# A two-layer conv / RG-LRU / pooling backbone on one core: modulation sums per column group, blocks turned by VectorE, and a new order in the first head

## The chip, the core and the metric

The kernel runs on one core of a Trainium2 chip. The core has five engines, each with a queue of its own: TensorE (PE, matrix products; its weight loads are shown apart as PEld), VectorE (DVE), ScalarE (ACT), GpSimd (POOL) and SyncE (SP, which here issues nearly all DMA transfers). They work side by side and wait for each other through semaphores. SBUF is the working memory with 128 partitions, PSUM the memory that PE writes its products to. The metric is the device time of one execution in microseconds (us); three runs are given by their median.

## The reference

1024 latent tokens and 256 context tokens of width 1024 pass an even layer (convolution branch and RG-LRU branch), then the latents pass an odd layer (pooling mixer). All data are float32. Each layer starts with an RMS norm and a modulation by vectors made from the conditioning `c` (for the context from `c_ctx`):

```python
shift, scale, gate = jnp.split(silu(c) @ mod_w[l] + mod_b[l], 3, axis=-1)
hx = rmsnorm(x, norm_g[l]) * (1 + scale) + shift       # latents
hc = the same for ctx with silu(c_ctx)                 # first layer only
z  = hx @ w_in                       # split in va, vg, ga, xb, gb
y_a = silu(layernorm(conv31(va * sigmoid(vg)))) * silu(ga)
u = conv4(xb); r, i = sigmoid(u @ w_r + b_r), sigmoid(u @ w_i + b_i)   # per head
y_b = (scan forwards + scan backwards, from the context's last states) * silu(gb)
x = x + gate * (concat(y_a, y_b) @ w_out)
```

The change concerns how `shift` and `scale` of the first layer are computed, how `hx` is formed from them, and the order of the work in the first of the eight heads of the even layer.

## The kernel before

**Layout.** Everything lies feature-major: a tile has 128 features on the partitions and tokens along the free side, so x is eight tiles `xs[k]` of 128x1024, used in two halves of 512 tokens. A product is exact to about float32 by splitting each operand into a high part (a cast to the matmul's reduced float32 type, `wh`, `gh`, `h0h`) and a low part (what is left, `wl`, `gl`, `h0l`), and adding high x high, high x low and low x high: three matmuls per tile (`mm3_steps`, line 153; `mm3_fixed`, line 686).

**Opening (lines 294 to 665).** Here the order on every engine is written by hand. `mm` (line 133) chains all matmuls, `load` (line 123) chains all DMA issues on SP, and `A` and `V` (class `Written`, line 106) chain the operations of ACT and VectorE. So each engine runs its work in the order of the program text, and an instruction that waits holds up what is behind it.

PE's opening work is the fold: eight products `fold_all(n, 0)` and `fold_all(n, 1)`, 24 matmuls each pair, which prepare weights of the second layer (`wfold`) and depend on the weights alone. ACT casts a weight (`cast`), VectorE takes its low part (`low`), ACT copies the product out of PSUM (`fold_copy`), and SP stores it (`fold_store`). Between the folds the inputs are prepared:

- `x_square` and `x_add` sum the squares of x; `ms` (a 128x32 stationary of ones, on four groups of 32 PSUM partitions) and `rx` make the row of reciprocal roots, which stays in two PSUM banks.
- The modulation sums. `cpad` holds silu of `c` and `c_ctx` as columns 0 and 1 of 32 (the rest zero), for each of eight tiles k of the contraction. PE's 128 output partitions are used as four groups of 32, each with its own stationary.
- `x_scale(k)` multiplies x by the scale and `rx` (VectorE, two halves), `x_high(k)` adds the shift and rounds (ACT), `x_low(k)` makes the low part (VectorE).

The sums go in four groups b of two feature tiles. `mod_load(b)` loads four blocks of `modW`; in `mod_mm(b)` the four partition groups share the contraction: group i takes tiles k = i and k = 4 + i, so each group ends with a partial sum for all columns. `mod_row(b)` copies the 128x512 result to SBUF (ACT), and `mod_turn(b)` is four matmuls with the copied row as stationary and a constant selector (`col(O_SEL, 2)`, two columns of `small`), which add the four partial sums and put features on partitions in one step (`modt`). `mod_cols(b)` adds the bias and makes `m0` (shift, scale and, later, gate, for both conditionings) and `a0` (norm gain times 1 + scale).

After the folds comes the first product, `xb0` = tile 0 of `xb`, 48 matmuls in two halves. On PE's queue, 39 matmuls into it, stands one that sums the context's squares (`ms_c`, line 634, tile `ssqc`), for which VectorE adds seven `csq` tiles after the last `x_low`. Then `cx` (the context) is normalised and modulated, and split into `cth` and `ctl` by ACT and VectorE. Still in the opening, `decay_exp` runs on ACT, and six gate dots on VectorE: a row block of `modT` times `cL` (silu of `c` on all partitions), summed along the free side into `m0`.

**Heads (lines 907 to 1000).** The order is again fixed on each engine, by `on` (line 670). In head j PE runs `vg` (two halves), in head 0 the context part `xc` of `xb`, `va` (two halves), the context part of the next `xb`, then the gate products of this head mixed with the next `xb`. ACT makes `first_tap`, VectorE `other_taps` of the 4-wide convolution into `uc`; `uh` and `ul` are its high and low part. `raw_split` (line 705) splits the next weights: high part on ACT, low part on POOL. `fill(n)` lets VectorE go on with the 31-wide convolution of a finished head; in head 0 there is none to go on with until the two products `u` = va * sigmoid(vg) exist. In head 0 the last two gate dots, the bias of the gates and `decay_rates` (26 small POOL operations and a reciprocal, for `chalf` and `cneg`, which the recurrence of the next head uses) come between `ul` and `va`. The splits of the next weight and of the gate weight stand behind these lines:

```python
            cast(uh, uc)
            act(sg[1], vg[1], AF.Sigmoid)
            fill(2)
            vec(nc.vector.tensor_tensor, out=ul, in0=uc, in1=uh.bitcast(F32), op=sub)
```

**Afterwards** come the products `gb` and `wob`, layer norm, `ga`, and the second layer (from line 1345 on), where a planner orders the instructions of each engine by priority and its own estimate of time, with a few orders given by hand.

Of the kernel before, what the change touches and what calls it, by code (L numbers as in the profile page):

```python
# [44 lines left out]
O_SEL = O_FG + KT  # L45
N_SM = O_SEL + 2

NB = 4
KB = KT // NB
MC = KB * P  # L50
# [6 lines left out]
def body(ctx, tc, xT, ctxT, cc, ccol, modT, modW, win, gw, wout, wu, grp, wg, wo1, small, edge, ident, outT):  # L57
# [136 lines left out]
    def decay_exp(act):  # L194
        act.activation(sa, lam, AF.Abs)
        act.activation(sa, sa, AF.Exp, scale=-1.0)
# [97 lines left out]
    with ExitStack() as sctx:  # L294
# [88 lines left out]
        modraw, modr, rows, modt = {}, {}, {}, {}  # L383

        def mod_load(b):
            for q in range(4):
                modraw[b, q] = dtile(f"modw_{b}_{q}") if b < 3 else ctile(f"modw_{b}_{q}", F32)
                load(modraw[b, q], modW[b, q])

        def mod_mm(b):  # L390
            modr[b] = psum(f"modr_{b}")
            for q in range(4):
                j, half = divmod(q, 2)
                for i in range(4):
                    mm(modr[b][32 * i : 32 * i + 32, j * MC : (j + 1) * MC], cpad[:, 4 * half + i],
                       modraw[b, q][:, i * MC : (i + 1) * MC], start=(q == 0), stop=(q == 3), skip_group_check=True)

        def mod_row(b):
            rows[b] = ttile(f"modrow_{b}")
            A.copy(rows[b], modr[b])  # L400

        def mod_turn(b):
            modt[b] = psum(f"modt_{b}")[:, : 4 * KB].rearrange("p (m c) -> p m c", c=2)
            for m in range(2 * KB):
                mm(modt[b][:, m], rows[b][:, m * P : (m + 1) * P], col(O_SEL, 2), start=True, stop=True)

        def mod_cols(b):
            for j in range(2):
                ms = slice(j * KT + KB * b, j * KT + KB * (b + 1))
                V.tensor_tensor(out=m0[:, :, ms], in0=modt[b][:, KB * j : KB * (j + 1)].rearrange("p m c -> p c m"),  # L410
                                in1=col(O_MB + ms.start, KB).unsqueeze(1).to_broadcast([P, 2, KB]), op=add)
            for k in range(KB * b, KB * (b + 1)):
                mod_scale(m0, a0, 0, k, V)
# [3 lines left out]
        def x_scale(k):  # L417
            for h in range(2):
                v = xs[k][:, HALF[h]]
                V.scalar_tensor_tensor(out=v, in0=v, scalar=a0[:, 0, k : k + 1], in1=rx[h], op0=mult, op1=mult)  # L420
# [1628 lines left out]
```

## Time and profile before

| what | us |
|---|---|
| median of 3 runs (1283.83 to 1284.45) | 1284.26 |
| the profiled execution | 1282.08 |
| its span, first to last instruction | 1280.3 |
| PE busy in the span | 1258.5 |
| DVE busy | 1134.8 |
| ACT busy | 654.9 |
| POOL busy | 296.9 |

All times inside the trace count from the start of the span. In the profile's lines L116 is the helper through which ACT and VectorE are chained in the opening, L137 the one for matmuls, L127 the one for DMA issues, and L674 the one for the heads, so operations are told apart by the tile that they write (left of `<-`) and read (right of it): `modr` and `modt` are the modulation's sums and turns, `modw` its weights, `x<-x,a,rx` is `x_scale`, `h0h` and `h0l` are `x_high` and `x_low`, `mod<-mod,cL` is a gate dot, `xbc` the context part of `xb`. In brackets stands how long the engine was idle before the line, and what ended that. A float32 matmul of the modulation (not split) shows as two records. In the chain of waits each piece of time is put down to what released the next.

### The profile page before, as it was taken

What the parts mean: (1) busy time and instruction counts of PE and PEld (TensorE: products, weight loads), DVE (VectorE), ACT (ScalarE), POOL (GpSimd) and SP (SyncE); (2) the same over time, 40 slices, a digit from 0 to 9 for tenths busy, and PEclk for the clock granted to TensorE, in tenths of its full rate; (3) what the DMA queues carried; (4) which work ended last, traced back from release to release, by engine and by line L of the source; (5) the groups of instructions that cost most, each with busy time, mean ns of one, the idle gap of its engine ahead of it and who ended that gap; (6) DMA issues with size and microseconds to landing.
All of it is one profiled execution on the core that took longest, in us unless ns stands there. A gap on an engine that the chain in (4) does not pass through costs nothing.

```text
span 1280.3 us, 16129 instructions
## 1 busy us (share of the span) xinstructions
PE 1258.5 (98%) x5822; PEld 1038.9 (81%) x5822; DVE 1134.8 (89%) x1747; ACT 654.9 (51%) x955; POOL 296.9 (23%) x173
## 2 busy tenths in 40 slices
PE   9999999999999999999999999999999999999997
PEld 7787888888888888888887878788888888788786
DVE  7789999999999999988959958999999987887876
ACT  8544566656666533237435346644343444644642
POOL 0005464446444557433210023000000000000003
PEclk9999999999999999999999999999999999999998
DMA  9961121112121234442418565334333334868723
GB/s 374 373 239 50 42 75 42 66 41 75 42 82 42 82 124 135 153 140 83 164 46 291 175 206 172 108 123 157 122 102 132 115 123 132 277 227 282 275 73 132
DMA packets 78704, 182.27 MB, mean 142 GB/s; under 512 B 7712, under 2 KB 23328, under 8 KB 78624
## 3 DMA queue, kind: packets, MB, share of 16 engines
q1 hardware_dynamic: 69632, 176.53, 39.7%
q10 hardware_dynamic: 8992, 4.72, 1.3%
q8 instruction: 45, 0.74, 0.2%
q14 instruction: 35, 0.29, 0.1%
HBM read 137.18 MB, written 44.04 MB: 142 GB/s over the span
## 4 chain that ended last, share of the span: by engine, by line
PE 63%; DVE 19%; DMA 8%; issue 3%; ACT 3%; POOL 2%; SPq 0%; POOLq 0%; ACTq 0%; DVEq 0%
PE wob L674 7%; PE fold L137 5%; DVE conv L674 5%; PE xb L674 4%; PE va L674 4%; PE vg L674 4%; DVE l L674 3%; PE g L674 3%; PE ga L674 2%; PE ga L158 2%; PE ga L160 2%; PE ga L159 2%; PE gb L674 2%; DMA yr_b<-y_b 1%; PE qb_g L1142 1%
## 5 line engine op out<-in xcount | busy, mean ns | idle before, releaser
L674 DVE SCALAR_TENSOR_TENSOR conv<-u,sm,conv 128x505 f32<-128x505 f32 (+6 forms) x224 | 153.7, 745 | 1.0
L1782 POOL TENSOR_TENSOR o<-x,rr 128x256 f32<-128x256 f32 (+1 forms) x10 | 9.7, 1005 | 443.1 <-ACT rr L1782 440.3
L674 ACT ACTIVATE l<-g,sm 128x512 f32<-128x512 f32 (+1 forms) x96 | 58.5, 618 | 57.6 <-PE g L674 57.0
L674 POOL TENSOR_TENSOR l<-l,l 128x1280 f32<-128x1280 f32 x16 | 47.1, 2964 | 25.6 <-ACT l L674 15.1
L674 PE MATMUL gb<-h0h,wl_gb 128*128 128x512 f32 x128 | 49.9, 390 | 0.3 <-POOL wl_gb L674 0.3
L674 PE MATMUL va<-h0h,wl_va 128*128 128x512 f32 x128 | 49.9, 390 | 0.2 <-POOL wl_va L674 0.2
L674 PE MATMUL gb<-h0h,wh_gb 128*128 128x512 f32 x128 | 49.9, 390 | 0.0
L674 PE MATMUL gb<-h0l,wh_gb 128*128 128x512 f32 x128 | 49.9, 389 | 0.0
L674 PE MATMUL va<-h0h,wh_va 128*128 128x512 f32 x128 | 49.8, 389 | 0.0
L674 PE MATMUL va<-h0l,wh_va 128*128 128x512 f32 x128 | 49.8, 389 | 0.0
L674 PE MATMUL wob<-ybl,wh_wob 128*128 128x512 f32 x128 | 49.8, 389 | 0.0
L674 PE MATMUL wob<-ybh,wl_wob 128*128 128x512 f32 x128 | 49.8, 389 | 0.0
L674 PE MATMUL wob<-ybh,wh_wob 128*128 128x512 f32 x128 | 49.8, 389 | 0.0
L674 DVE TENSOR_TENSOR_SCAN l<-l,l 128x256 f32<-128x256 f32 (+1 forms) x32 | 48.7, 1522 | 1.1
L674 DVE SCALAR_TENSOR_TENSOR conv<-cL,wsum,conv 128x506 f32<-128x506 f32 (+3 forms) x70 | 48.1, 744 | 0.2
L674 POOL TENSOR_TENSOR l<-l,uc 128x1280 f32<-128x1280 f32 x16 | 47.7, 3001 | 0.0
L103 ACT CAST wq_wo<-wr_wo 128x512 fp32r<-128x512 f32 x48 | 28.7, 620 | 36.6 <-DMA wr_wo<-wo 17.9
L103 ACT CAST wq_g<-wr_g 128x512 fp32r<-128x512 f32 x48 | 28.2, 620 | 35.7 <-DVE wr_g L1120 16.8
L104 POOL TENSOR_TENSOR wl_wu<-wr_wu,wh_wu 128x1024 fp32r<-128x1024 f32 x8 | 19.2, 2396 | 110.8 <-ACT wh_wu L103 110.8
L674 PE MATMUL xb<-h0l,wh_xb 128*128 128x512 f32 x112 | 43.8, 391 | 0.0
L674 PE MATMUL xb<-h0h,wh_xb 128*128 128x512 f32 x112 | 43.8, 391 | 0.0
L674 PE MATMUL vg<-h0l,wh_vg 128*128 128x512 f32 x112 | 43.6, 389 | 0.0
(619 smaller groups left out, 4357.4 us busy)
## 6 DMA issues: line engine op xcount, KB each, us to landing
modw<-modW SPq DMA_DIRECT2D x16, 512.0 KB, 10.4
x_part<-xp SPq DMA_DIRECT2D x32, 256.0 KB, 2.3
mod<-modT SPq DMA_DIRECT2D x32, 256.0 KB, 4.1
wr_v<-wfold SPq DMA_DIRECT2D x16, 512.0 KB, 4.1
wr_g<-wg SPq DMA_DIRECT2D x16, 512.0 KB, 4.4
wr_wo<-wo SPq DMA_DIRECT2D x16, 512.0 KB, 4.3
mod<-modT SPq DMA_DIRECT2D x14, 512.0 KB, 4.9
yr_t<-y_t SPq DMA_DIRECT2D x14, 512.0 KB, 6.4
```

The source lines that it names most:

```text
L103: return (nc.scalar.copy(hi, src), eng.tensor_tensor(out=lo, in0=src, in1=hi.bitcast(F32), op=sub))
L104: eng.tensor_tensor(out=lo, in0=src, in1=hi.bitcast(F32), op=sub))
L137: m = nc.tensor.matmul(*args, **kw)
L158: mm(ps, hi[:, kc], xh[k][:, cols], start=(k == 0), stop=False)
L159: mm(ps, hi[:, kc], xl[k][:, cols], start=False, stop=False)
L160: mm(ps, lo[:, kc], xh[k][:, cols], start=False, stop=(k == ks - 1))
L674: last[eng] = f(*args, **kw)
L1142: mm = nc.tensor.matmul(ps, lo, xh[k], start=False, stop=(k == KH - 1), skip_group_check=not first)
L1782: tail[eng] = f(*args, **kw)
```

## The change

It has three parts.

1. **Whole sums per column group.** Each partition group of PE now owns 32 of the 128 columns of a feature tile and runs over all eight k, so its sum is whole. `modr` then holds, in group i, column block i in row 0 (`c`) and row 1 (`c_ctx`); turning each 32x32 block puts features on partitions. VectorE does that straight from PSUM (`V.transpose`), so the ACT copy, the four selector matmuls, the selector's columns and four PSUM tiles go. The groups are now two, two and four feature tiles (three groups instead of four): 32, 32 and 32 matmuls with 128, 128 and 256 moving columns, where there were four times 16 with 256. The third group's sums run in three pieces between folds. `modW` is laid out anew: 16 blocks of 512 KB as before. On SP, `fold_store(0)` moves ahead of blocks 8 to 11; `w_load(6)` stays between block 11 and block 12.
2. **Last inputs by halves.** For tiles 4 to 7 the first token half of `x_scale`, `x_high` and `x_low` is made for all four tiles ahead of the last folds, the second half after them. `x_high` and `x_low` of tiles 1 and 3 move ahead of the following fold pieces; `fold_copy` and the casts of weights 6 to 8 stand at new places between them.
3. **First head.** The last operations of the opening's ACT and VectorE chains are now linked to the head's. `ctx_split`, `decay_exp` and the split of `va`'s weight follow `first_tap`; the six opening dots are issued in the head (two after `other_taps`, one between `uh` and `ul`, three after `ul`), the last two with the bias and `decay_rates` after the two `u`. The next weight and the gate weight `gw` are split ahead of `uh`. The loads of `modT` keep their order on SP.

```diff
+        def mod_mm(b, qs):
+            k0, n = ((0, 2), (2, 2), (4, 4))[b]
+            w = n * 64
+            if b not in modr:
+                modr[b] = psum(f"modr_{b}")
+            for q in qs:
+                for e in range(4 // n):
+                    k = (q % 4) * 2 + e if n == 2 else q - 8
+                    for i in range(4):
+                        c = (4 * e + i) * w
+                        mm(modr[b][32 * i : 32 * i + 32, :w], cpad[:, k], modraw[q][:, c : c + w],
+                           start=(k == 0), stop=(k == KT - 1), skip_group_check=True)
 
         def mod_cols(b):
+            k0, n = ((0, 2), (2, 2), (4, 4))[b]
+            t = ttile(f"modt_{b}")[:, : n * 64]
+            V.transpose(out=t, in_=modr[b][:, : n * 64])
...
+        for q in range(4, 8):
+            mod_load(q)
+        fold_store(0)
+        for q in range(8, 12):
+            mod_load(q)
+        w_load(6)
+        for q in range(12, 16):
+            mod_load(q)
...
-        mod_mm(0)
-        mod_row(0)
-        fold_all(4, 1, 0, 1)
-        mod_turn(0)
-        fold_store(0)
-        w_load(6)
-        mod_load(3)
+        mod_mm(0, range(4))
         mod_cols(0)
         x_scale(0)
         x_scale(1)
         x_high(0)
-        fold_all(4, 1, 1, 4)
+        fold_all(4, 1)
         fold_copy(4, 1)
+        x_high(1)
         x_low(0)
...
+        mod_mm(2, range(12, 14))
         fold_all(6, 0, 0, 2)
+        mod_mm(2, range(14, 16))
         mod_cols(2)
         cast(A, 7)
+        fold_all(6, 0, 2, 4)
+        x_scale(4, (0,))
+        x_high(4, HALF[0])
+        x_scale(5, (0,))
+        fold_copy(6, 0)
+        x_high(5, HALF[0])
+        x_low(4, HALF[0])
         low(7)
...
         fold_all(7, 0)
+        for k in range(4, 8):
+            x_scale(k, (1,))
+            x_high(k, HALF[1])
+            if k == 4:
+                fold_copy(7, 0)
+            else:
+                x_low(k - 1, HALF[1])
+        x_low(7, HALF[1])
         fold_all(7, 1)
...
+                fill(2)
+            first_tap(j, xb, uc[:, C:])
+            if state is None:
+                ctx_split()
+                decay_exp()
                 wva = raw_split(raw_va0, "va0")
             other_taps(j, xb, uc[:, C:], 1)
+            if state is None:
+                for m in range(2):
+                    gate_dot(2 * KT + m, gate_raw[m])
...
             if state is None:
                 for m in range(3 * KT - 2, 3 * KT):
+                    gate_raw.append(L[m % 6][:, :D])
+                    nc.sync.dma_start(gate_raw[-1], modT[0, m])
+                cast(uh, uc)
+                act(sg[1], vg[1], AF.Sigmoid)
+                gate_dot(2 * KT + 2, gate_raw[2])
+                vec(nc.vector.tensor_tensor, out=ul, in0=uc, in1=uh.bitcast(F32), op=sub)
+                for m in range(3, 6):
+                    gate_dot(2 * KT + m, gate_raw[m])
...
             whole_[0] = j + 1
+            if state is None:
+                for m in range(3 * KT - 2, 3 * KT):
+                    gate_dot(m, gate_raw[m - 2 * KT])
+                vec(nc.vector.tensor_tensor, out=m0[:, 0, 2 * KT :], in0=m0[:, 0, 2 * KT :],
+                    in1=col(O_MB + 2 * KT, KT), op=add)
+                decay_rates()
```

More of the change, by code (lines that the diff above doesn't have):

```diff
@@ L398, in mod_row, with mod_load @@
[L398 to L405, printed above, removed]
+        modraw, modr = {}, {}
+        def mod_load(q):
+            modraw[q] = dtile(f"modw_{q}") if q < 12 else ctile(f"modw_{q}", F32)
+            load(modraw[q], modW[q])
```

164 lines of the change are left out of this document (61 added, 103 removed).

## The prediction

> **What bounds the kernel now.** I read the page first, then busy time by stage, then the chain of waits through the first 110 us, and last the timelines of the engines there.
>
> ```profile
> span 1280.3 us, 16129 instructions
> PE 1258.5 (98%) x5822; PEld 1038.9 (81%) x5822; DVE 1134.8 (89%) x1747; ACT 654.9 (51%) x955; POOL 296.9 (23%) x173
> ```
>
> Busy time by stage (columns: stretch, its length, busy time of PE, weight loads, DVE, ACT, POOL, granted clock, DMA share, GB/s):
>
> ```profile
> 0.00:60.00 60.00, 57.78 (x380) 44.71 (x381) 45.55 (x79) 41.20 (x60) 0.20 (x4) 1.00 0.98 374
> 60.00:90.00 30.00, 30.00 (x144) 24.87 (x142) 25.47 (x37) 17.55 (x25) 2.30 (x1) 1.00 0.80 294
> 90.00:120.00 30.00, 27.03 (x134) 22.80 (x134) 28.10 (x41) 10.31 (x17) 12.20 (x29) 1.00 0.14 45
> ```
>
> PE bounds the kernel: it is idle 22 us in 1280. Everything that the change touches lies before 120 us. There PE idles only at the start and between 90 and 120 us; what else can be won must be matmul time. So a microsecond counts only if PE executes it or waits for it. The clock is full in all three stretches. In the first one the DMA engines are as full as PE (0.98).
>
> Chain of waits (start, length, what):
>
> ```profile
> 25.66 0.57 PE ms_x L137 x16
> ...
> 33.04 1.86 PE modr L137 x32
> 34.90 0.91 PE fold L137 x3
> 35.81 0.85 PE modt L137 x8
> 36.66 2.19 PE fold L137 x9
> ...
> 51.77 1.86 PE modr L137 x32
> ...
> 54.53 0.87 PE modt L137 x8
> 55.40 8.97 PE fold L137 x39
> 64.38 8.99 PE xb L137 x39
> 73.36 0.45 PE ms_c L137 x2
> ```
>
> Four modulation sums (modr) and four turns (modt) stand on PE in the chain, between fold matmuls, ahead of the first product xb.
>
> PE's own timeline in the first head (start, length; what it waited for in brackets):
>
> ```profile
> 89.70 0.40 PE L674 MATMUL va<-h0l,wh_va 128*128 128x512 f32 x1
> 90.31 0.50 PE L674 MATMUL va<-h0h,wl_va 128*128 128x512 f32 x1 [0.21 <-POOL wl_va L674]
> ...
> 100.97 0.28 PE L674 MATMUL xbc<-ctl,wh_xb 128*128 128x256 f32 x1
> 104.00 0.39 PE L674 MATMUL xbc<-cth,wl_xb 128*128 128x256 f32 x1 [2.75 <-POOL wl_xb L674]
> ```
>
> Here are the two other stalls: PE waits for POOL's low parts of two weights, wl_va and, much longer, wl_xb.
>
> **The change part by part.** I count in PE time, negative for a gain.
>
> *Turns leave PE: -3.37.* The four modt runs go (first and last above, 0.85 and 0.87; with the two between them 3.37). VectorE's block transposes replace them. The before trace has none; its nearest rows are VectorE operations from PSUM on 512 columns (0.68 each, below) for blocks of 128, 128 and 256 columns. I take 0.2, 0.2 and 0.4, between a fixed 0.1 and the full 0.68. They follow modr directly, so ACT's four copies of modr and the second trip through PE are gone as well, and the last one delays the x steps by 0.4 at most. [...]
>
> *Narrower sums: +0.84.* Columns streamed are equal: 64 matmuls of 256 before, 64 of 128 and 32 of 256 after. Before, 32 records take 1.86, or 58 ns each. The shape of the new 128-wide ones (32 stationary columns, 128 moving) is that of ms_x: 16 records in 0.57, 36 ns each. Two groups of 64 such records are 4.56, the third (64 of 58 ns) is 3.72; together 8.28 against 4x1.86 = 7.44. Ends: 0 if only columns count, +3.7 if each narrow record costs a wide one's 58 ns. I take ms_x, which is the same shape.
>
> [...]
>
> *Fewer breaks: -0.55.* Twelve folds beside a modr and a modt take 0.91+2.19 = 3.10, where 8.97/39 = 0.23 each makes 2.76; a break costs some 0.18. Eight go down to five, since group 2 runs in three pieces. Ends: -1.0 to 0.
>
> *The transfers hold part of it: +0.45.*
>
> ```profile
> 24.12 9.69 SPq L127 DMA_DIRECT2D modw<-modW  x8
> ...
> 37.32 4.25 SPq L127 DMA_DIRECT2D modw<-modW  x4
> ...
> DMA to landing us min/median/max: 9.3/10.4/10.8
> ```
>
> The first four blocks are in by then; these rows are the issues of blocks 4 to 11 and 12 to 15, then the time from issue to landing. Issues take up to the landing of older ones, as the DMA engines are full: block 11 goes out at 33.5 and lands near 43.9, block 15 goes out at 41.2 and lands near 51.6. Before, PE came for that group at 51.77: just in time. The change leaves the bytes ahead of it the same (it only moves fold_store(0) ahead of blocks 8 to 11, and w_load(6) stays behind those), so it still lands at 51.6, while PE would now reach that block at 51.4; blocks 8 to 11 land one store later (512 KB, 1.4 us at 374 GB/s), the last near 45.3, when PE comes at 44.9. I count 0.45 for both; ends 0 and 1.0. In return the earlier store frees its buffer: the following wait of ACT goes, off PE's path.
>
> ```profile
> 45.27 0.59 ACT L116 COPY fo<-fold 128x512 f32<-128x512 f32 x1 [2.85 <-DMA wfold<-fo]
> ```
>
> Sum of the stage: -3.37+0.84-0.55+0.45 = -2.6; the first product starts near 61.8 instead of 64.38.
>
> *Inputs by halves: +0.3.* VectorE does not get shorter with this.
>
> ```profile
> 39.81 1.28 DVE L116 SCALAR_TENSOR_TENSOR h0l<-x,m,h0h 128x1024 fp32r<-128x1024 f32 x1
> 51.15 2.73 DVE L116 SCALAR_TENSOR_TENSOR x<-x,a,rx 128x512 f32<-128x512 f32 x4
> 65.74 3.59 DVE L116 TENSOR_TENSOR ssqc<-ssqc,csq 128x256 f32<-128x256 f32 x7
> 69.25 1.22 DVE L116 TENSOR_TENSOR wl<-wr,wh 128x1024 fp32r<-128x1024 f32 x1
> ```
>
> After the last group's columns (52.2 on PE, near 53.0 on VectorE) stand 16 half operations of 0.68, two low parts of 1.22, and some 1.2 of waiting for ACT (one such wait, of 1.50, is shown with rival a): 14.5, to 67.5. First halves and wl_8 come just in time for xb (62.0 against 61.8 plus 0.45 until the first low matmul). The second halves (67.5) are needed only from tile 4 of the second half, near 70. But ms_c, 8.99 into xb on PE's queue at 70.8, needs the seven context sums behind them: 67.5+3.59 = 71.1. PE, with the rest of xb queued behind, waits 0.3, where it had 4 us of slack (69.3 against 73.36). From here each late microsecond of VectorE costs one of PE. Ends: 0 and +9 (the slow rival).
>
> ACT's side of it (start, length):
>
> ```profile
> 56.72 1.16 ACT L116 ACTIVATE h0h<-x,m 128x1024 fp32r<-128x1024 f32 x1
> ...
> 66.23 1.44 ACT L116 ACTIVATE csq<-cx 128x256 f32<-128x256 f32 x4
> ...
> 86.57 1.05 ACT L674 CAST wh_va<-wr 128x1024 fp32r<-128x1024 f32 x1 [2.76 <-PE vg L674]
> ```
>
> ACT makes a half high part in 0.6 and a square in 0.36, faster than VectorE uses them; its sixteen steps fit beside.
>
> *The first head, wl_xb: -2.9.* Before, ACT cast wh_xb only after uh, which waited for VectorE's taps, which stood behind six gate dots; POOL began wl_xb at 100.60 and PE lost 104.00-100.97-0.12 = 2.9. Now both weights (with gw) are split ahead of uh, and two dots stand ahead of the context taps, the rest behind uh or the two u products. wl_xb can start when ACT has done the context tap, near 89, and end near 92; PE needs it near 98.7. The stall goes whole. Late next are ul and the gate weights: two dots, taps and ul on VectorE end near 96, PE asks at 101. The dots moved behind the u products and the decay rates on POOL behind them feed only the tanh of the next head and, far later, the gating. VectorE enters the convolution some 4 us earlier than before, PE 4.6. That lag is absorbed (columns: who waits for whom, total us, times, longest):
>
> ```profile
> DVE uc L674 <- ACT uc L674: 4.0, 7, 1.0
> DVE u L674 <- PE va L674: 2.9, 4, 0.9
> ```
>
> In the heads VectorE waits 6.9 us for PE and its followers.
>
> *wl_va: +0.6.* VectorE's timeline, then POOL's (start, length):
>
> ```profile
> 80.99 2.43 DVE L116 TENSOR_TENSOR ctl<-cx,cth 128x1024 fp32r<-128x1024 f32 x2
> ...
> 86.78 1.22 DVE L116 SCALAR_TENSOR_TENSOR mod<-mod,cL 128x1024 f32<-128x1024 f32 x1
> ...
> 87.92 3.41 DVE L116 SCALAR_TENSOR_TENSOR mod<-mod,cL 128x1024 f32<-128x1024 f32 x1
> ...
> 92.41 3.91 DVE L674 SCALAR_TENSOR_TENSOR uc<-xb,sm,uc 128x1022 f32<-128x1022 f32 x3
> ```
>
> ```profile
> 87.70 2.55 POOL L674 TENSOR_TENSOR wl_va<-wr,wh_va 128x1024 fp32r<-128x1024 f32 x1 [87.26 <-ACT wh_va L674]
> 100.60 3.35 POOL L674 TENSOR_TENSOR wl_xb<-wr_xb,wh_xb 128x1024 fp32r<-128x1024 f32 x1 [10.35 <-ACT wh_xb L674]
> ```
>
> A dot takes 1.2, but the one issued beside wl_va took 3.41: a dot and a POOL split do not run together, whoever is first holds the other up. Counted from ms_c (73.36), VectorE ends ctl at +10.1 and, in the new order, the taps (3.9) at +14.0, where two dots follow. POOL starts wl_va at +14.3, since wh_va's cast waits for the weight buffer that vg holds to its end (ACT's last row above). So a dot probably gets in first and POOL starts 0.8 later, less the 0.15 it lost before: +0.6. Ends: -0.4 (the present stall goes) and +1.5.
>
> Moved at no cost: context casts and decay_exp behind first_tap on ACT. They get their cx when VectorE has it, after that tap; ctl then ends 3 us ahead of xc's need. If the tap waited for space, up to those 3 us are cover. The mod0 loads keep their place on SP.
>
> Total: -2.6+0.3-2.9+0.6 = -4.6. The profiled execution took 1282.08 (span 1280.3 and 1.8 around it), so it would be 1277.5; the median of the runs, 1284.26, stands 2.2 above it, so the prediction is 1279.6.
>
> **The rivals.** (a) *Taking turns, slower.* ACT and VectorE hand each half to and fro. If each step waited for the other, 53.0 is followed by 8 halves of 0.68+0.6+0.68, two low parts, a cast of 1.05 and the squares alternating with the sums (0.36+0.51, seven times): 53.0+15.7+2.4+1.1+6.1 = 78.3 against 70.8. PE stands at ms_c 7.5 instead of 0.3, and three fold copies of 0.59 on ACT add 1.8: 1279.6+7.2+1.8 = 1288.6. It makes the kernel slower from a VectorE delay of 4.9 on. For it: VectorE does wait for ACT (the row below). Against: the order writes two scales ahead between most pairs.
>
> ```profile
> 55.37 1.28 DVE L116 SCALAR_TENSOR_TENSOR h0l<-x,m,h0h 128x1024 fp32r<-128x1024 f32 x1 [1.50 <-ACT h0h L116]
> ```
>
> (b) *The first gain stops at ms_c.* A milder form: wl_7, wl_8 or the sums are 2 to 3 us late, and PE waits for what the turns gave back: 1282.2.
>
> (c) *The split's place is taken.* wl_xb is early, but dots and splits alternate so that ul or wl_gw comes after 101, or two dots hold wl_va: 2 of the 2.9 come back, 1281.6.
>
> (d) *Better.* No ms_c wait, no transfer wait, only columns count, and the va stall goes too: 1279.6-0.3-0.45-0.84-1.0 = 1277.0.
>
> **How the numbers follow.** Changes under 0.2% (2.6 us) can't be told from none here. The forecast, 1278.3 to 1281, gets 0.60; (a) 0.09; (b) 0.14, mostly inside 0.2%; (c) 0.08, half of it; (d) 0.09. Faster, below 1281.7: 0.60+0.09+0.04+0.05 = 0.78. Slower: 0.09. Same: 0.13. The range runs from (d), 1277.0, to 1283.0, past (b); it leaves out (a) and the worst of (b).
>
> **What would show it.** Right: no modt, three transposes under 0.7; xb's start near 61.8; no wait of PE for wl_xb; gate matmuls some 4.6 us earlier. Wrong: PE waiting at ms_c for the sums, at wl_7 or wl_8, or more than 0.5 at wl_va; modr runs of 128 columns above 2.3. From the second layer on (590 us) no order is written by hand; new waits of PE there could move the end by a microsecond or two, either way.

## The result and the profile after

| | before | after |
|---|---|---|
| median, us | 1284.45 (1283.83 to 1288.64, 5 runs) | 1276.51 (1273.26 to 1278.22, 5 runs) |
| the profiled execution / its span, us | 1282.08 / 1280.3 | 1273.26 / 1271.4 |

The five runs of the kernel before include the three of the table ahead. The ratio (of the runs' means) is 0.9923, interval 0.9899 to 0.9946. The forecast was 1279.6 with a range from 1277.0 to 1283.0: the sign was right, the gain was larger, and the time lies 0.5 us below the range. Measured twice more, on two chips, the same kernel gave 0.9950 and 0.9946 (below).

The page of the kernel after, first the span, then busy time by engine:

```profile
span 1271.4 us, 16188 instructions
...
PE 1253.4 (99%) x5854; PEld 1035.9 (81%) x5854; DVE 1135.8 (89%) x1747; ACT 654.9 (52%) x955; POOL 298.1 (23%) x173
```

Busy time by stage of the kernel after (columns as in the prediction):

```profile
0.00:60.00 60.00, 57.94 (x423) 45.20 (x424) 45.83 (x76) 40.32 (x59) 0.20 (x4) 1.00 0.99 381
60.00:90.00 30.00, 28.77 (x137) 23.73 (x136) 28.17 (x38) 19.78 (x30) 3.66 (x2) 1.00 0.80 283
90.00:120.00 30.00, 30.00 (x150) 25.50 (x150) 29.75 (x49) 11.08 (x17) 14.24 (x29) 1.00 0.13 43
```

PE is now busy through the whole of 90 to 120 us; the 3.0 us of idle time there are gone, and 1.2 us have appeared between 60 and 90. Over the whole trace PE's busy time fell by 5.1 us and the span by 8.9.

The chain of waits of the kernel after (start, length, what) shows where the 1.2 us come from:

```profile
44.76 0.64 PE modr L132 x8
45.40 2.94 PE fold L132 x12
48.34 1.00 PE modr L132 x16
49.35 1.60 PE fold L132 x6
50.95 1.00 PE modr L132 x16
...
70.65 0.43 DVE ssqc L111
71.08 0.14 issue
71.22 0.67 PE ms_c L132 x2
```

No turn stands on PE any more, and the context's squares (`ssqc`) now lead to `ms_c` on the chain. In this kernel L111, L132 and L671 are the helpers that were L116, L137 and L674 before.

PE's timeline in the kernel after (start, length; what it waited for in brackets):

```profile
33.14 1.96 PE L132 MATMUL modr<-modw,cpad 128*32 128x128 f32 x64
38.69 1.96 PE L132 MATMUL modr<-modw,cpad 128*32 128x128 f32 x64
...
44.76 0.64 PE L132 MATMUL modr<-modw,cpad 128*32 128x256 f32 x8 [0.43 <-DMA modw<-modW]
...
71.22 0.67 PE L132 MATMUL ms_c<-ssqc,ones 128*128 128x256 f32 x2 [0.61 <-DVE ssqc L111]
...
88.78 0.50 PE L671 MATMUL va<-h0h,wl_va 128*128 128x512 f32 x1 [0.62 <-POOL wl_va L671]
...
99.58 0.28 PE L671 MATMUL xbc<-cth,wl_xb 128*128 128x256 f32 x1
...
102.22 0.28 PE L671 MATMUL g<-uh,wh_gw 128*128 128x256 f32 x1
```

VectorE and POOL of the kernel after, in the opening and the first head:

```profile
35.46 0.31 DVE L111 STREAM_TRANSPOSE modt<-modr 128x128 f32<-128x128 f32 x1
...
52.02 0.45 DVE L111 STREAM_TRANSPOSE modt<-modr 128x256 f32<-128x256 f32 x1 [3.22 <-PE modr L132]
...
85.27 1.22 DVE L671 SCALAR_TENSOR_TENSOR mod<-mod,cL 128x1024 f32<-128x1024 f32 x1
...
86.41 3.40 DVE L671 SCALAR_TENSOR_TENSOR mod<-mod,cL 128x1024 f32<-128x1024 f32 x1
```

```profile
85.76 2.96 POOL L671 TENSOR_TENSOR wl_va<-wr,wh_va 128x1024 fp32r<-128x1024 f32 x1 [85.32 <-ACT wh_va L671]
89.31 2.77 POOL L671 TENSOR_TENSOR wl_xb<-wr_xb,wh_xb 128x1024 fp32r<-128x1024 f32 x1 [0.58 <-ACT wh_xb L671]
```

Setting the start of the same PE row in both traces side by side tells where the time went:

| first row of | before | after | difference |
|---|---|---|---|
| `modr` | 32.97 | 33.14 | +0.17 |
| `xb` of tile 0 | 64.21 | 61.59 | -2.62 |
| `ms_c` | 73.20 | 71.22 | -1.98 |
| `xbc` for head 1 | 100.85 | 99.34 | -1.51 |
| gates of head 0 | 106.74 | 102.22 | -4.52 |
| `vg` of head 1 | 124.59 | 120.06 | -4.53 |
| second layer, `wq_woa` | 671.78 | 667.35 | -4.43 |
| `wh_wu` fold | 748.09 | 743.36 | -4.73 |
| `wq_g` | 814.66 | 807.96 | -6.70 |
| last PE row ends | 1272.03 | 1263.12 | -8.91 |

Up to 672 us the forecast (gates 4.6 us earlier, a plain shift behind them) holds within 0.2. In this pair of traces, half of the gain comes behind 740 us, where the change touches nothing: from the gates of the first head on, every engine has the same instructions in the same order in both programs.

One place behind 740 us can be read at once. Kernel before, PE's timeline and then the granted clock (third from last in a stage row):

```profile
751.18 0.53 PE L137 MATMUL fold<-gh,wh_wu 128*128 128x512 f32 x1 [2.00 <-ACT wh_wu L103]
```

```profile
751.00:755.00 4.00, 3.82 (x10) 3.00 (x11) 3.13 (x2) 2.01 (x4) 2.38 (x1) 0.57 0.47 159
```

The same place in the kernel after:

```profile
746.59 0.50 PE L132 MATMUL fold<-gh,wh_wu 128*128 128x512 f32 x1 [2.13 <-ACT wh_wu L98]
```

```profile
747.00:751.00 4.00, 4.00 (x19) 3.29 (x18) 3.80 (x3) 1.64 (x3) 2.65 (x2) 1.00 0.49 156
```

Both wait about 2 us for a weight whose cast came late. Before, the granted clock then fell to 0.57 and PE ran 10 matmuls in 4 us; after, it stayed at 1.00 and PE ran 19. Does that differ by chance from execution to execution, or does the change bring it? And are the two parts of the change worth what the first 120 us say?

### The profile page after: what moved, and what is told of

Read it like the earlier page. It is cut to its first block, busy times and chain, and to the rows that moved or that the text cites. A ratio compares the mean times of both kernels' runs of the same rounds, so it can differ in the third digit from the quotient of the medians.

```text
span 1271.4 us, 16188 instructions
## 1 busy us (share of the span) xinstructions
PE 1253.4 (99%) x5854; PEld 1035.9 (81%) x5854; DVE 1135.8 (89%) x1747; ACT 654.9 (52%) x955; POOL 298.1 (23%) x173
## 4 chain that ended last, share of the span: by engine, by line
PE 61%; DVE 19%; DMA 12%; ACT 3%; issue 3%; POOL 2%; SPq 0%; POOLq 0%; DVEq 0%; ACTq 0%
PE wob L671 7%; PE vg L671 5%; PE va L671 5%; DVE conv L671 5%; PE xb L671 4%; DVE l L671 3%; PE g L671 3%; DMA x_part<-xp 2%; PE ga L671 2%; PE ga L153 2%; PE ga L154 2%; DMA graw<-grp 2%; PE gb L671 2%; PE ga L155 2%; DMA modw<-modW 2%
## 5 line engine op out<-in xcount | busy, mean ns | idle before, releaser
L671 DVE SCALAR_TENSOR_TENSOR conv<-u,sm,conv 128x505 f32<-128x505 f32 (+6 forms) x224 | 153.6, 744 | 1.0
L671 ACT ACTIVATE l<-g,sm 128x512 f32<-128x512 f32 (+1 forms) x96 | 58.6, 618 | 57.8 <-PE g L671 57.0
L671 POOL TENSOR_TENSOR l<-l,l 128x1280 f32<-128x1280 f32 x16 | 47.1, 2964 | 25.6 <-ACT l L671 15.1
L671 PE MATMUL va<-h0h,wl_va 128*128 128x512 f32 x128 | 49.9, 390 | 0.6 <-POOL wl_va L671 0.6
L671 PE MATMUL gb<-h0h,wl_gb 128*128 128x512 f32 x128 | 49.9, 390 | 0.4 <-POOL wl_gb L671 0.4
L671 PE MATMUL gb<-h0h,wh_gb 128*128 128x512 f32 x128 | 49.8, 389 | 0.0
L671 PE MATMUL gb<-h0l,wh_gb 128*128 128x512 f32 x128 | 49.8, 389 | 0.0
L671 PE MATMUL va<-h0l,wh_va 128*128 128x512 f32 x128 | 49.8, 389 | 0.0
L671 PE MATMUL va<-h0h,wh_va 128*128 128x512 f32 x128 | 49.8, 389 | 0.0
L671 PE MATMUL wob<-ybh,wh_wob 128*128 128x512 f32 x128 | 49.8, 389 | 0.0
L671 PE MATMUL wob<-ybl,wh_wob 128*128 128x512 f32 x128 | 49.8, 389 | 0.0
L671 PE MATMUL wob<-ybh,wl_wob 128*128 128x512 f32 x128 | 49.8, 389 | 0.0
L671 DVE TENSOR_TENSOR_SCAN l<-l,l 128x256 f32<-128x256 f32 (+1 forms) x32 | 48.7, 1521 | 1.1
L671 DVE SCALAR_TENSOR_TENSOR conv<-cL,wsum,conv 128x506 f32<-128x506 f32 (+3 forms) x70 | 48.1, 745 | 0.2
L671 POOL TENSOR_TENSOR l<-l,uc 128x1280 f32<-128x1280 f32 x16 | 47.7, 3000 | 0.0
L671 PE MATMUL xb<-h0l,wh_xb 128*128 128x512 f32 x112 | 43.8, 391 | 0.0
L671 PE MATMUL xb<-h0h,wh_xb 128*128 128x512 f32 x112 | 43.8, 391 | 0.0
L671 PE MATMUL xb<-h0h,wl_xb 128*128 128x512 f32 x112 | 43.6, 389 | 0.0
L671 PE MATMUL vg<-h0h,wh_vg 128*128 128x512 f32 x112 | 43.6, 389 | 0.0
```

The lines of the kernel that those rows point to most:

```text
L671: last[eng] = f(*args, **kw)
```

## The experiments

**Theory A**: the change gives what the first 120 us show, 4.6 us, and the rest is drawn anew in each execution by waits for late transfers in the second layer and by half-clock stretches behind them. **Theory B**: the wait for `wl_xb` costs more than its length, since the clock falls behind it. **Theory C**: the changed program has a shorter second layer.

**One part alone.** `head_only` is the kernel before with part 3 of the change, `open_only` the one with parts 1 and 2. The core of the edits:

```diff
# head_only: against before
+            first_tap(j, xb, uc[:, C:])
+            if state is None:
+                ctx_split()
+                decay_exp()
                 wva = raw_split(raw_va0, "va0")
...
+                cast(uh, uc)
+                act(sg[1], vg[1], AF.Sigmoid)
+                gate_dot(2 * KT + 2, gate_raw[2])
...
# open_only: against before
-        mod_mm(0)
-        mod_row(0)
...
-        mod_turn(0)
...
+        mod_mm(0, range(4))
         mod_cols(0)
...
+        x_scale(4, (0,))
+        x_high(4, HALF[0])
```

> The kernel before with the third part of the change alone (order of casts, splits and gate dots in the first head). By the trace the 2.9 us wait of PE for wl_xb goes and the wait for wl_va grows by some 0.5: gate matmuls of the first head 2.4 us earlier than before, time about 1282. If the part of the measured gain that the first 120 us do not show (some 3.5 of 7.9 us) belongs to this part, the time is 1278 to 1279 instead.

> The kernel before with the first two parts alone (whole sums, turns on VectorE, inputs by halves). By the trace ms_c runs 2.0 us earlier and everything behind it keeps its distance, the wait for wl_xb among it: time about 1282.4. If the rest of the measured gain belongs to these parts, 1279. The two parts together should make what the whole change makes by then, 4.4 us.

Measured: `head_only` 1279.9 us, ratio 0.9970 (0.9958 to 0.9983); `open_only` 1280.6, ratio 0.9968 (0.9952 to 0.9984). PE's timeline of `head_only`:

```profile
91.55 0.50 PE L677 MATMUL va<-h0h,wl_va 128*128 128x512 f32 x1 [0.59 <-POOL wl_va L677]
...
102.35 0.28 PE L677 MATMUL xbc<-cth,wl_xb 128*128 128x256 f32 x1
```

The wait for `wl_xb` is gone, that for `wl_va` is 0.4 longer: from `modr` to the gates this part gives 2.63. In `open_only` the stretch from `modr` to `xb` is 2.79 shorter than before, but the gates, counted from `modr`, come only 1.01 earlier (at 106.94 in its trace). At `ms_c` 0.63 are lost again; PE's timeline and the stages behind it show the rest:

```profile
103.11 0.39 PE L668 MATMUL xbc<-cth,wl_xb 128*128 128x256 f32 x1 [2.72 <-POOL wl_xb L668]
```

```profile
103.00:104.00 1.00, 0.89 (x7) 0.89 (x8) 1.00 (x1) 0.00 (x0) 1.00 (x2) 1.00 0.00 0
104.00:105.00 1.00, 1.00 (x8) 1.00 (x7) 0.97 (x3) 0.00 (x0) 1.00 (x1) 0.70 0.63 197
105.00:106.00 1.00, 1.00 (x7) 1.00 (x6) 0.76 (x3) 0.00 (x0) 0.63 (x3) 0.50 0.81 324
106.00:107.00 1.00, 1.00 (x7) 1.00 (x6) 0.96 (x3) 0.00 (x0) 0.76 (x5) 0.50 0.48 111
107.00:108.00 1.00, 1.00 (x6) 0.96 (x6) 1.00 (x4) 0.75 (x2) 0.83 (x3) 0.60 0.97 348
```

A little over a microsecond after the wait the granted clock falls to half for 3.4 us. In this execution the wait cost its 2.7 and some 1.4 more: fifteen matmuls of 256 columns 0.21 apart instead of 0.12. This is theory B, in one execution. The two parts' gains, 3.8 and 4.1 us of 1284, each exceed their share of the first 120 us (2.3 each by the forecast's terms). Both intervals (2.2 to 5.4 and 2.1 to 6.2 us) still reach that share, so this only says that neither part alone is seen to bring the surplus.

**The changed kernel again, twice, and the kernel before again.** No edit.

> The changed kernel once more, for a second trace. Theory A, chance in the second layer (the length from the first head's gate matmuls to the end differs from one execution to the next, by waits and by the clock after a wait): this length differs from the 1169.0 us of the first trace by 1 to 4 us, and the lost time stands at other places. Theory B, the gain behind 120 us is the change's own: the length is 1169 to 1170 again, against 1173.4 before.

> The changed kernel once more, beside the one with 40 matmuls. If the gain is the 4.6 us of the first head alone: ratio 0.9964 (0.995 to 0.9978). If later waits add to it as in the two pairs of runs so far: 0.993 to 0.995, and the time from the last matmul group of the first head to the end is 1143 to 1146 against 1147.

> The kernel before, unchanged, for a second trace of it. If every execution draws its own late transfers and half-clock stretches, its median stands within 0.2% of the kernel before (ratio 0.998 to 1.002), and its trace repeats the first 100 us of the first trace within 1 us, with the 2.7 us wait for wl_xb, but differs from it by 1 to 4 us between the last matmul group of the first head and the end (1147.4 there), with waits and half-clock stretches at other places. If the kernel before always runs into the same half-clock stretch (behind the wait of 2.0 us near 749), that stretch of 1.5 us stands in this trace too, at the same place.

Measured: `after_again` 1276.95, ratio 0.9950 (0.9930 to 0.9969); `after_third` 1276.49, ratio 0.9946 (0.9930 to 0.9963); `before_again` 1282.94, ratio 0.9998 (0.9981 to 1.0016). The gates come 4.04 and 4.30 us earlier than in the first trace of before; counted from the start of `modr`, 4.51 and 4.73 (4.69 in the first trace). So the first 120 us repeat. In the trace of `after_third` it stays so to the end: 4.21 us less at the last PE row, as theory A has it. The ratios do not follow theory A: 4.6 us alone would be 0.9964, and all three measured ones are lower. What differs between the traces is, among other waits, what happens near 748 us. `before_again`, PE's timeline and the stage behind:

```profile
750.17 0.50 PE L137 MATMUL fold<-gh,wh_wu 128*128 128x512 f32 x1 [1.37 <-ACT wh_wu L103]
```

```profile
751.00:755.00 4.00, 4.00 (x19) 3.32 (x18) 3.49 (x3) 0.17 (x1) 1.59 (x1) 1.00 0.74 231
```

`after_third`, the same:

```profile
746.81 0.79 PE L132 MATMUL fold<-gh,wh_wu 128*128 128x512 f32 x1 [1.99 <-ACT wh_wu L98]
```

```profile
747.00:751.00 4.00, 4.00 (x11) 3.19 (x12) 3.12 (x2) 1.86 (x3) 2.37 (x2) 0.59 0.49 167
```

Now the kernel before has no fall and the changed one has it: it differs from execution to execution and is not brought by the change. The wait for `wl_xb` in `before_again` (2.72 us) had no fall behind it either.

**The wait filled with work.** `before_warm` gives PE twelve matmuls whose result nobody reads, where it waited for `wl_xb`:

```diff
+                if state is None:
+                    pad = psum("pad")
+                    for _ in range(12):
+                        on("pe", nc.tensor.matmul, pad, ones_r, hh[0][:, HALF[0]], start=True, stop=True)
                 xc = psum(f"xbc{j + 1}")[:, :C]
```

> The kernel before with 12 matmuls of 128x512 whose result nobody reads (2.7 us of PE) ahead of the context part of the next xb in the first head, so that PE works where it waited for wl_xb. If that wait costs only its length, the work takes its place: gate matmuls at the same time (106.7 less the difference of the start of modr, within 0.3), ratio 0.999 to 1.001. If the wait also brings the clock to half behind it in a good part of the executions, the median falls by 0.6 to 1.5 us (ratio 0.9988 to 0.9995) and no half-clock stretch is seen near 105 in the trace.

Measured: 1283.06, ratio 0.9998 (0.9987 to 1.0009), and the gates, counted from `modr`, at 73.82 against 73.77: the work took the place of the wait. A mean cost of the fall of up to 1.7 us a run (the interval's lower end) isn't excluded, but none is seen. As an average, theory B is worth little here; the next pair shows what it is worth when it strikes.

**How long a wait brings the half clock.** Ahead of the gates of all eight heads PE waits for a small matmul's result to pass a chain of casts on ACT (nine casts in `wait_long`, three in `wait_short`); only the matmul that waits reads the tile `late`, and nothing uses its result.

```diff
+            on("pe", nc.tensor.matmul, pad[:, :112], ones_r, hh[0][:, :112], start=True, stop=True)
+            cast(late_, pad[:, :112])
+            for _ in range(8):         # wait_short: 2
+                cast(late_, late_.bitcast(F32))
+            pad = psum(f"late{j}")
+            on("pe", nc.tensor.matmul, pad[:, :112], ones_r, late_, start=True, stop=True)
```

> The changed kernel with a wait of PE of some 2.5 us ahead of the gate matmuls in each of the eight heads (a matmul, nine small copies on ACT in a row, a matmul that reads the last; nobody uses the result). Theory 'a wait costs itself': the time grows by 8 x 2.5 = 20 us, all matmuls behind run at 0.227 us each. Theory 'the clock falls behind some waits': behind some of the eight the matmuls run at half speed for some us, as behind the 2.0 us wait in the second layer of the first trace and behind wl_xb's wait in open_only, and each such fall adds 1.5 to 1.7 us.

> As wait_long, with three small copies instead of nine: waits of about 1 us in eight heads. Theory 'the clock falls behind some waits': it depends on the length, and none or few of the eight fall. Theory 'any wait': as many as with the long ones.

Measured: `wait_long` 1322.63, ratio 1.0303 (1.0286 to 1.0321); `wait_short` 1293.77 (one run). The waits of PE in `wait_long` (total, times, longest), then its stages around the first:

```profile
PE late L671 <- ACT late L671: 26.2, 8, 3.3
```

```profile
104.00:107.00 3.00, 1.18 (x5) 1.18 (x6) 2.93 (x6) 1.61 (x6) 2.24 (x11) 0.57 0.01 3
107.00:110.00 3.00, 3.00 (x9) 2.32 (x8) 3.00 (x6) 0.83 (x2) 2.32 (x10) 0.50 0.00 0
110.00:113.00 3.00, 3.00 (x12) 2.39 (x11) 3.00 (x6) 1.01 (x2) 0.77 (x4) 0.79 0.00 0
```

PE's timeline of `wait_short` and the stage behind:

```profile
104.17 0.32 PE L671 MATMUL late<-late,ones_r 128*128 128x112 f32 x1 [1.38 <-ACT late L671]
```

```profile
105.00:108.00 3.00, 3.00 (x15) 2.49 (x14) 2.93 (x7) 1.44 (x3) 2.15 (x10) 1.00 0.00 0
```

Half clock (steps of 0.43 instead of 0.23) came with all eight waits of `wait_long`, seven of 3.3 us and one of 2.9 (with the first it began 1.4 us before the wait ended, and lasted twice as long), and with none of the eight of 1.0 to 1.4 in `wait_short`. At the first row of `gb`, behind the heads, `wait_short` stands 14.7 us later than the changed kernel with 11.0 of these waits, so the added steps cost 3.7 besides; `wait_long` stands 41.8 later, and 41.8 - 26.2 - 3.7 leaves 11.9, or 1.5 for each wait, of slow matmuls (an estimate; it takes the added steps to cost the same in both). Between these lengths the length alone does not decide: waits of 1.78 (`after_pad_h7`), 1.81 (`after_pad30`), 1.94 (`whole`), 1.99 (`after_third`), 2.00 (before) and 2.25 us (`after_pad40`) in the second layer, and the 2.72 of `open_only`, had a fall; 1.79 and 1.89 (`wait_short`), 1.96 (`after_pad30`), 2.13 (after), 2.72 (`before_again`) and 2.75 (before, `wl_xb`) had none.

What decides can be read from the traces. Each stretch of half clock lasts 3.41 us or twice that, but for a longer one that ends each trace, and all that a trace has start whole multiples of 3.413 us apart (in `wait_long` 15, 14, 14, 14, 14, 14, 13 and 119 of them; in the kernel before 152, from 751.52 to the last one at 1270.34). So in these traces the falls lie on a grid of time, and what counts in them is how much of a wait lies between two lines of it. Here are the two waits for `wl_xb`, of 2.75 us in the kernel before and of 2.72 in `open_only`, each cut along the grid of its own trace (behind the length stands PE's busy time):

```profile
99.57:102.98 3.41, 1.68 (x9) 1.24 (x7) 3.41 (x4) 1.47 (x3) 2.38 (x1) 1.00 0.00 0
102.98:106.39 3.41, 2.39 (x20) 2.39 (x21) 3.19 (x3) 0.00 (x0) 3.41 (x3) 1.00 0.36 115
```

```profile
100.98:104.39 3.41, 1.28 (x10) 1.28 (x11) 3.38 (x3) 0.00 (x0) 3.41 (x2) 1.00 0.06 12
104.39:107.80 3.41, 3.41 (x18) 3.41 (x17) 3.13 (x8) 0.56 (x1) 2.71 (x8) 0.50 0.74 256
```

Before, a line of the grid cuts the wait: PE is idle for 1.73 us of one stretch and 1.02 of the next, and nothing falls. In `open_only` 2.13 us lie in one stretch, and the next has half clock. Over all seventeen traces, more than 1.79 us of idle time in a stretch at full clock was followed by half clock in 16 of 16 cases and less than 1.64 in none; from 1.64 to 1.79 there were two with and five without. The last fall of each trace is left out of this count: it comes among or just behind the last matmuls, many of them of a single column, after 0.6 to 1.6 us of idle time by the records, so the count holds for streams of wide matmuls only. Two short waits can add up: in `after_pad` a fall at 809.62 stands behind waits of 0.94 and 0.91 us in one stretch.

**A delay in place of the gain.** The changed kernel with useless matmuls ahead of the first head's gates, 10, 20, 30 and 40 of them (2.25, 4.5, 6.75 and 9.0 us), and with 20 in the last head (`after_pad_h7`):

```diff
+            if state is None:          # after_pad_h7: if final
+                pad = psum("pad")
+                for _ in range(20):    # after_pad10, 30, 40: 10, 30, 40
+                    on("pe", nc.tensor.matmul, pad, ones_r, hh[0][:, HALF[0]], start=True, stop=True)
```

> The changed kernel with 20 matmuls of no use (128x512, 0.227 us each, 4.5 us together) on PE ahead of the first head's gate matmuls, so that the heads start when they did before. They write to a tile that nobody reads. Theory A (chance behind 120 us) or B' (the second layer's waits depend on when it starts): within 1 us of the kernel before, apart from its spread. Theory C (something in the changed program, its buffers or its layout in memory, makes the second layer shorter): 3 to 4 us faster than before, that is the changed kernel and 4.5.

> The changed kernel with 40 useless matmuls of 128x512 (9.0 us) ahead of the first head's gates, twice as many as before, in the same place. If time in the first head only shifts what follows, the time is that of the changed kernel on this chip plus 9.0 (some 1285.5 to 1286.5, ratio to the kernel before 1.001 to 1.002). If the extra 3 us that 20 such matmuls cost were a price of standing late against the transfers of the second layer, the surplus stays or grows: 1288 to 1290, ratio 1.003 to 1.005.

> The changed kernel with 10 useless matmuls of 128x512 (2.25 us) ahead of the first head's gates. The changed kernel alone stood at 1276.5, 4.5 us of such work at 1284.6 and 9.0 at 1284.8. If the surplus grows evenly with the delay: 1276.5+2.25+1.7 = 1280.5, ratio 0.9972. If it is a step: 1278.8 (ratio 0.9960) before it or 1281.8 (0.9983) behind it. If only the executions drawn so far made it: 1278.8 too.

> The same with 30 useless matmuls (6.75 us). A smooth line through 4.5 and 9.0 gives 1284.7 (ratio 1.0008). If the delay only shifts what follows, and the 4.5 us case was drawn high: 1283.3 (0.9997). If waits in the second layer hang on the phase in no simple order, it may fall anywhere from 1281 to 1287.

> The same 20 useless matmuls (4.5 us) in the last head instead of the first, near 375 us. If the surplus hangs on when the second layer begins against the transfers, wherever the delay comes from: as in the first head, 1284.6 (ratio 1.0007). If it hangs on the first head itself: 1276.5+4.5 = 1281.0 (0.9977).

| delay, us | ratio to before (interval) | as us of 1284 | less the delay |
|---|---|---|---|
| 0, `after_again` | 0.9950 (0.9930 to 0.9969) | -6.4 | -6.4 |
| 0, `after_third` | 0.9946 (0.9930 to 0.9963) | -6.9 | -6.9 |
| 2.25 | 0.9962 (0.9946 to 0.9977) | -4.9 | -7.1 |
| 4.5 | 1.0008 (0.9994 to 1.0022) | +1.0 | -3.5 |
| 4.5, last head | 0.9997 (0.9984 to 1.0009) | -0.4 | -4.9 |
| 6.75 | 0.9988 (0.9976 to 1.0000) | -1.5 | -8.3 |
| 9.0 | 1.0009 (0.9996 to 1.0022) | +1.2 | -7.8 |

A delay costs about its length: from 0 to 9.0 us the time grows by 7.6 to 8.1. But the two kernels with 4.5 us stand some 4 and 2 us above that line, and where the delay lies makes no difference that the intervals could tell. So the surplus does not grow with the delay, it is not a step either (6.75 is below 4.5), and the place of the delay does not decide. With the padding at 4.5 us the second layer begins when it does in the kernel before (`wq_woa` at 672.75 and 671.83, before 671.78), and in that position it is as slow as before's. Theory C falls in its plain form: the changed program at that position does not have a shorter second layer.

How far one and the same second layer varies is seen from `wq_woa` to the end of each profiled execution: 605.9, 607.8 and 610.2 (the changed kernel's three), 610.3 and 610.8 (before's two), 608.1, 612.0, 611.5 and 608.7 (delays of 2.25 to 9.0 in the first head), 612.3 (last head). As far as `wq_woa`, PE keeps step in these traces within 0.6 us, counted from `vg` of head 1 (547.1 to 547.7; the last-head delay left aside); behind that, waits of PE, most of them for casts and low parts of freshly loaded weights, differ in place and length from trace to trace. Behind `wq_woa` PE is idle for 6.0, 6.2 and 7.9 us in the changed kernel's three traces, 8.1 and 9.2 in before's two, 10.4 and 8.4 with 4.5 us of delay, and 8.0, 8.0 and 6.6 with 2.25, 6.75 and 9.0; and there are none, one or two falls, at some 1.6 us each (eight matmuls 0.42 apart instead of 0.23). Without both, 589.6 to 591.5 us are left up to PE's last row, so these two make most of the range.

**By halves or whole.** `whole` is the changed kernel with part 2 undone for tiles 4 to 7, the places of the casts and copies between them included.

```diff
+        x_scale(4)
+        x_scale(5)
+        fold_all(6, 0, 2, 4)
+        x_high(4)
+        x_low(4)
         cast(A, 7)
-        fold_all(6, 0, 2, 4)
-        x_scale(4, (0,))
-        x_high(4, HALF[0])
-        x_scale(5, (0,))
...
-        x_low(4, HALF[0])
```

> The changed kernel with whole tiles for inputs 4 to 7 (the second part undone there, the steps in the order of the kernel before). If the halves are what lets PE keep the time won by the turns, low parts 7 and 8 come late: waits of about 1 us each in the last folds and at the first product, which then starts some 2 us later than in the changed kernel; ms_c has no wait, so that 1.4 us of it stay: time 1.4 us above the changed kernel. If the halves are worth nothing, the same time.

Measured: 1277.73, ratio 0.9958 (0.9945 to 0.9972). PE's waits in its opening:

```profile
56.94 0.50 PE L132 MATMUL fold<-gh,wh 128*128 128x512 f32 x1 [0.32 <-ACT wh L111]
...
58.46 0.50 PE L132 MATMUL fold<-gh,wl 128*128 128x512 f32 x1 [0.79 <-DVE wl L111]
...
64.76 0.50 PE L132 MATMUL xb<-h0h,wl 128*128 128x512 f32 x1 [0.56 <-DVE wl L111]
```

Without the halves VectorE and ACT make the last weights late: counted from `modr`, `xb` starts at 30.08 (28.45 with them) and the gates at 70.70 (69.08). So the halves and their order, costed in the prediction as a loss of 0.3 by themselves, carry 1.6 of the 2.8 us by which `xb` comes earlier. The total (1277.7 against 1276.5) shows 1.2 of it, within the scatter.

**Two waits taken away.** `tuned` is the changed kernel with the low part of `va`'s weight made on VectorE ahead of the first dots, and with `ms_c` three steps further back on PE's queue.

```diff
-        for _ in range(KT + 5):
+        for _ in range(KT + 8):
...
-                wva = raw_split(raw_va0, "va0")
+                wva = [wpool.tile([P, D], F32R, tag=v, name=f"{v}_va0") for v in ("wh", "wl")]
+                cast(wva[0], raw_va0)
             other_taps(j, xb, uc[:, C:], 1)
             if state is None:
+                vec(nc.vector.tensor_tensor, out=wva[1], in0=raw_va0, in1=wva[0].bitcast(F32), op=sub)
```

> The changed kernel with its two new waits of PE taken away: the low part of va's weight in the first head is made by VectorE (1.2 us) ahead of the gate dots, not by POOL (2.4 us, held up by a dot); and ms_c stands three steps later in xb on PE's queue, so that the context's sums are there. By the trace the waits of 0.6 each go: 1.2 us faster than the changed kernel, 5.6 to 6 us faster than before by the first 120 us. If VectorE, now 1.2 us later in the first head, were the bound, nothing would be won.

Measured: 1273.36 (1273.18 to 1276.41), ratio 0.9927 (0.9913 to 0.9941), the best median of all kernels here; but the changed kernel's own three ratios run from 0.9923 to 0.9950, so the two can't be told apart by the time. PE's timeline, then VectorE's:

```profile
87.79 0.50 PE L671 MATMUL va<-h0h,wl_va 128*128 128x512 f32 x1 [0.38 <-DVE wl_va L671]
```

```profile
86.52 1.22 DVE L671 TENSOR_TENSOR wl_va<-wr,wh_va 128x1024 fp32r<-128x1024 f32 x1
```

The wait at `ms_c` is gone, that at `wl_va` is 0.38 instead of 0.62, and the gates, counted from `modr`, start 1.07 earlier than in the changed kernel (68.01 against 69.08).

## Why the prediction was right and where it failed

**Turns, sums, breaks and transfers: right, in sum.** Counted from `modr`, `xb` came 2.79 us earlier (2.60 and 2.83 in the other two traces); the forecast was 2.6. This was partly luck, since two sizes that were off cancelled (next paragraph). The transposes took 0.31, 0.31 and 0.45 where 0.2, 0.2 and 0.4 were taken, off PE's path. The block that lands last of group 8 to 11 held PE 0.43 at 44.76, where 0.45 was counted for it and block 15 together; block 15 made no wait.

**Narrower sums: mis-sized.** The prediction took +0.84 from the spacing of `ms_x`. From the start of a group of 64 narrow records to the next fold pass 1.88 us (33.14 to 35.02), against 1.86 for 32 wide ones (32.97 to 34.83): 64 records more, with the same columns in all, cost 0.04 for both groups together, the lower end of the prediction's bounds. With the breaks (-0.55 in the prediction) the two terms were to be +0.29; what is left of -2.79 after the turns (-3.37) and the wait (0.43) is +0.15, so some +0.1 for the breaks: 0.8 too much in one term made up for 0.65 too little in the other. The three pieces of the third group cost their breaks: 16 records took 1.00, 0.07 more than at 58 ns each.

**Inputs by halves: right mechanism, 0.64 instead of 0.3.** VectorE's squares ended late for `ms_c`, at the place named: 0.61 of waiting. What the prediction did not say is that without the halves the gates would have come 1.6 later (`whole`).

**`wl_va`: right, 0.41 instead of 0.6.** A dot got in first (1.22), the second ran beside POOL's split and took 3.40, the split itself took 2.96 where it took 2.55 before, and PE waited 0.62 instead of 0.21.

**`wl_xb`: right as a mean, -3.0 for -2.9.** The wait is gone in every trace with part 3. That such a wait can cost some 1.4 more (`open_only`) was not in it; with the wait filled with work, the time is the same within the interval (`before_warm`), so on average no more than its length is seen.

**The rivals.** Taking turns (a) did not happen: `ms_c` waits 0.61. Case (b) happened to that extent. (c) did not: nothing waits at the gates. (d), whose bound was crossed, did not happen either: the three waits that it takes away are there, and only its columns came true.

**The step that failed** is the last one: everything behind the first head was taken as a plain shift, to which new waits of PE could add "a microsecond or two", and the range's low end, 1277.0, was made of terms of the first 120 us alone. The shift itself is right up to 672 us, and to the end in one of three traces. But the second layer's own time, from identical instructions, ran over 6 us in the traces (605.9 to 612.3), from waits for late casts and from half-clock stretches that cost some 1.6 us each; and by its three ratios the changed kernel gained 6.4, 6.9 and 9.9 us (by the medians 7.3, 7.4 and 7.9), where the first 120 us give 4.5 to 4.7. So some 2 to 5 us of the gain were made in a part of the program that the prediction had put at nothing in its sum and its range. The range's low end should have stood lower by about half of those 6 us.

**What stays open**: why the kernels whose second layer begins at 672 to 673 us (before, and both with 4.5 us of padding) are some 3 us slower than the line through the others. With that stays open why the changed kernel gains more than its first 120 us. The position alone may not do it: in the trace of `open_only` the second layer begins at 672.77 (some 1.4 of it by the fall), and its ratio is 0.9968. Half clock alone does not do it either: it was seen in traces of both kinds. Whether it hangs on the phase against the transfers or on where the waits lie on the grid of 3.413 us was not tried.

## What to carry to other kernels

Cost an edit on the engine that bounds up to the next place where that engine waits for transfers, and behind that place give the forecast a range of its own: read it from how far repeated traces of one program differ there (here 6 us of 610), not from the edit. Work taken off the bounding engine can come back as a wait for the engine that took it unless its order is changed as well; here 1.6 of 2.8 us hung on making the last inputs by halves. And a wait of PE of some 2 us or more is worth removing ahead of several short ones of the same sum that lie further apart, for the half clock that may follow: here it came with all eight waits of 2.9 to 3.3 us and with none of eight of 1.0 to 1.4.

## What the runs showed of the hardware

- Half clock came with a wait of PE of 2.9 to 3.3 us in 8 of 8 cases (`wait_long`), with one of 1.0 to 1.4 in 0 of 8 (`wait_short`), and with one of 1.8 to 2.8 in some executions only (2.72 with it in `open_only`, 2.72 without in `before_again`). A stretch lasted 3.41 us or twice that, but for a longer one that ended each trace; within a trace they started whole multiples of 3.413 us apart. Over the seventeen traces half clock followed a stretch of that grid with more than 1.79 us of idle time in 16 of 16 cases, one with less than 1.64 in none (among wide matmuls). It cost 1.4 us in `open_only` and some 1.6 in the second layer.
- 64 matmul records with 32 stationary and 128 moving columns took 1.88 us (kernel after), 32 with 32 and 256 took 1.86 (kernel before).
- A 32x32 block transpose on VectorE straight from PSUM took 0.31 us for 128x128 and 0.45 for 128x256 float32 (kernel after).
